# Issuing two of a rotation kernel's three stores from ACT instead of SyncE

## The chip, the cores and the metric

The kernel runs on one core of one Trainium2 chip. The metric is the device time of one execution in microseconds. The kernel before took 121.96 us in the median of three runs, from 121.85 to 122.02 us.

## The reference

A batch of 96 images (32 times 3 channels) of 256 x 256 float32 values is turned by 180 degrees: each image is reversed in both of its axes, which is the same as reversing its 65,536 values in order.

```python
batch, c, h, w = 32, 3, 256, 256
x = np.random.randn(batch, c, h, w).astype(np.float32)
return np.rot90(x, k=2, axes=(-2, -1)).astype(np.float32)
```

So 25.17 MB are read from DRAM, turned, and 25.17 MB written back. There is no arithmetic.

## The kernel before

The 96 images are taken as three groups of 32. In a group each image is cut into four parts of E = 16,384 values, so that a group is a tile of 128 partitions (image and part) by 16,384 values, 64 KB on each partition and 8.39 MB in all. Three such tiles, A, Bt and Ct, hold the three groups; each has a place of its own, so no tile is used twice. A fourth, T, of 2,048 values per partition, is scratch.

Turning an image is done in two steps. The order of the four parts is reversed by the access pattern of a DMA, and the values within a part are reversed by VectorE (DVE) in place:

- Group 0, tile A: loaded as it is, turned by DVE, stored with the parts reversed (`store`, L56 and L57). The load is in two pieces: the first 512 columns are issued by ACT, the other 15,872 by SyncE (both recorded on L54).
- Group 1, tile Bt: loaded with the parts reversed (L69), turned by DVE, stored as it is (L79).
- Group 2, tile Ct: loaded as it is (L54), turned by DVE, stored with the parts reversed (L57).

All loads are issued at the start, in the order A, Bt, Ct. `turn` walks from both ends of a tile to its middle and calls `swap` for each pair of pieces; `swap` makes three reversed or plain copies on DVE (recorded on L49): the right piece reversed into T, the left piece reversed into the right one's place, T into the left one's place. A and Ct are turned in 4 such steps of 2,048 columns, which makes 12 copies each; Bt in 6 steps of 1,366 columns (the last of 1,362), which makes 18. The copies stay in the order of the program.

The order of the stores is that of the program too: Bt's store first, then A's, then, after the turn of Ct, Ct's. Each engine's queue is in order: an instruction that issues a DMA waits on its engine for the semaphores of the copies and loads that it needs, and whatever stands behind it on that engine waits as well. Each engine that issues DMAs has a queue of its own on the 16 DMA engines: the profile's q1 has the bytes that SyncE issued, its q10 those that ACT issued. The scheduling framework (Tile) puts in the semaphores, and the waits at the program's end, recorded on L108.

Of the kernel before, what the change touches and what calls it, by code (L numbers as in the profile page):

```python
# [2 lines left out]

os.environ.setdefault("NEURON_RT_ULTRASERVER_MODE", "4")

# [4 lines left out]


@with_exitstack
def kernel(
    ctx: ExitStack,
    tc: tile.TileContext,
    x: bass.AP,
    out: bass.AP,
):
    nc = tc.nc  # L20
    P = 128

    B, C, H, W = x.shape
    L = H * W
    G = 32
    E = L // 4
    J = E // 8

    x4 = x.rearrange("b c h w -> (b c) (h w)").rearrange(
        "(g n) (s e) -> g (n s) e", n=G, s=4)  # L30
    o4 = out.rearrange("b c h w -> (b c) (h w)").rearrange(
        "(g n) (s e) -> g n s e", n=G, s=4)

    xr = x.rearrange("b c h w -> (b c) (h w)").rearrange(
        "(g n) (s e) -> g n s e", n=G, s=4)
    of = out.rearrange("b c h w -> (b c) (h w)").rearrange(
        "(g n) (s e) -> g (n s) e", n=G, s=4)

    pool = ctx.enter_context(tc.tile_pool(name="slots", bufs=1))
    A = pool.tile([P, E], x.dtype, tag="A")  # L40
    Bt = pool.tile([P, E], x.dtype, tag="B")
    Ct = pool.tile([P, E], x.dtype, tag="C")
    T = pool.tile([P, J], x.dtype, tag="T")

    def back(t, lo, hi):
        return t[:, hi - 1:(lo - 1 if lo else None):-1]

    def copy(dst, src):
        c = nc.vector.tensor_copy(out=dst, in_=src)  # L49
        tc.keep_in_program_order(c)  # L50
        return c

    def load(t, g, lo=0, hi=E, queue=nc.sync):
        return queue.dma_start(out=t[:, lo:hi], in_=x4[g][:, lo:hi])  # L54

    def store(t, g):  # L56
        return nc.sync.dma_start(out=o4[g][:, ::-1, :], in_=t[:, :])  # L57

    def swap(t, lo, w):
        hi = E - lo - w  # L60
        copy(T[:, 0:w], back(t, hi, hi + w))
        copy(t[:, hi:hi + w], back(t, lo, lo + w))
        copy(t[:, lo:lo + w], T[:, 0:w])

    half = E // 2

    load(A, 0, 512, E)
    load(A, 0, 0, 512, nc.scalar)
    nc.sync.dma_start(out=Bt[:, :], in_=xr[1][:, ::-1, :])  # L69
    load(Ct, 2)  # L70

    def turn(t, pieces):
        step = -(-half // pieces)
        for lo in range(0, half, step):
            swap(t, lo, min(step, half - lo))

    turn(A, 4)
    turn(Bt, 6)
    nc.sync.dma_start(out=of[1], in_=Bt[:, :])  # L79
    store(A, 0)  # L80
    turn(Ct, 4)
    store(Ct, 2)


# [1 line left out]
_INS = ['x']  # L86
_OUTS = [((32, 3, 256, 256), 'float32')]


# [23 lines left out]
```

## Time and profile before

| | us |
|---|---|
| median of three runs | 121.96 |
| the profiled execution's own time | 121.85 |
| its span, from first to last instruction | 120.1 |
| DVE busy, in 42 copies | 45.2 |
| idle time of DVE before its first copy of A, of Bt, of Ct | 22.6, 4.3, 3.1 |

The span holds 1,008 DMA packets and 50.33 MB, in the mean 419 GB/s. The profile's page lists the busy share of each engine, the span in 40 slices (each digit is the busy share of a slice in tenths), the DMA queues, and each DMA issue with the time from its issue to its landing. A row of the timeline gives start and duration, engine, line, operation, and in brackets the idle time before it with what ended that. "SPq" and "ACTq" are the instruction queues of SyncE and ACT, which issue DMAs. The trace also has a record of each single DMA packet, with its start, duration, size and queue.

### The profile page before, as it was taken

The page shows a single profiled execution, that of the slowest core. Times are in us where ns is not written, and L with a number is a line of the kernel's source. Part 1 is how long each engine was busy: PE and PEld are TensorE (multiplying, and loading weights), DVE is VectorE, ACT ScalarE, POOL GpSimd, SP SyncE. Part 2 cuts the span into 40 slices and gives each one's busy share as a digit, 9 for nine tenths or more (in the row PEclk, how much of TensorE's full clock was granted, in tenths as well). Part 3 has the DMA queues.
Part 4 walks back from the last instruction along what each step waited for, and adds up shares of the span by engine and source line. Part 5 has one row for each costly group of instructions (what it writes and reads, how often), then busy time and mean ns, then how long its engine had stood idle before and what let it go on. Part 6 is the DMA issues. An engine that isn't in the chain of part 4 may idle for free.

```text
span 120.1 us, 100 instructions
## 1 busy us (share of the span) xinstructions
DVE 45.2 (38%) x42; POOL 0.2 (0%) x4
## 2 busy tenths in 40 slices
DVE  0000000499995099999459999400000000000000
POOL 0000000000000000000000000000000000000000
DMA  9888988898889988998899889988998889888980
GB/s 338 349 349 351 697 349 349 360 677 371 349 349 633 415 349 349 590 459 349 349 524 524 349 349 480 568 349 349 415 633 349 349 371 677 349 349 371 655 371 0
DMA packets 1008, 50.33 MB, mean 419 GB/s; under 512 B 112, under 2 KB 112, under 8 KB 240
## 3 DMA queue, kind: packets, MB, share of 16 engines
q1 hardware_dynamic: 864, 50.07, 96.9%
q10 hardware_dynamic: 144, 0.26, 0.6%
HBM read 25.17 MB, written 25.17 MB: 419 GB/s over the span
## 4 chain that ended last, share of the span: by engine, by line
DMA 34%; DVE 26%; another core or an unknown queue 3%; issue 1%; SPq 0%; DVEq 0%
DMA Bt<-in_x_dram 34%; DVE Bt L49 9%; DVE T L49 9%; DVE Ct L49 8%; SPq L54 0%; DVEq L49 0%
## 5 line engine op out<-in xcount | busy, mean ns | idle before, releaser
L49 DVE COPY T<-A 128x2048 f32<-128x2048 f32 x4 | 4.9, 1226 | 22.7 <-DMA A<-in_x_dram 22.6
L49 DVE COPY T<-Bt 128x1366 f32<-128x1366 f32 (+1 forms) x6 | 5.2, 874 | 4.5 <-DMA Bt<-in_x_dram 4.3
L49 DVE COPY T<-Ct 128x2048 f32<-128x2048 f32 x4 | 4.9, 1227 | 3.2 <-DMA Ct<-in_x_dram 3.1
L49 DVE COPY Bt<-T 128x1366 f32<-128x1366 f32 (+1 forms) x6 | 5.2, 873 | 0.2
L49 DVE COPY Bt<-Bt 128x1366 f32<-128x1366 f32 (+1 forms) x6 | 5.2, 872 | 0.2
L49 DVE COPY Ct<-T 128x2048 f32<-128x2048 f32 x4 | 4.9, 1227 | 0.1
L49 DVE COPY A<-T 128x2048 f32<-128x2048 f32 x4 | 4.9, 1227 | 0.1
L49 DVE COPY A<-A 128x2048 f32<-128x2048 f32 x4 | 4.9, 1227 | 0.1
L49 DVE COPY Ct<-Ct 128x2048 f32<-128x2048 f32 x4 | 4.9, 1227 | 0.1
L97 POOL MEMSET const-bfloat16-1.0<- 128x1 bf16 x1 | 0.1, 101 | 0.0
L97 POOL MEMSET const-uint8-127<- 128x1 uint8 x1 | 0.1, 101 | 0.0
L97 POOL MEMSET const-float32-0.0<- 128x1 f32 x1 | 0.1, 98 | 0.2 <-issue 0.2
L97 POOL MEMSET const-float32-1.0<- 128x1 f32 x1 | 0.1, 98 | 0.0
## 6 DMA issues: line engine op xcount, KB each, us to landing
A<-in_x_dram SPq DMA_DIRECT2D x1, 7936.0 KB, 21.8
A<-in_x_dram ACTq DMA_DIRECT2D x1, 256.0 KB, 22.0
Bt<-in_x_dram SPq DMA_DIRECT2D x1, 40.8
Ct<-in_x_dram SPq DMA_DIRECT2D x1, 59.5
out_dram<-Bt SPq DMA_DIRECT2D x1, 22.3
out_dram<-A SPq DMA_DIRECT2D x1, 41.2
out_dram<-Ct SPq DMA_DIRECT2D x1, 42.7
```

Source lines behind the costliest of these rows:

```text
L49: c = nc.vector.tensor_copy(out=dst, in_=src)
L97: nc = _bacc.Bacc("TRN2", target_bir_lowering=False, num_devices=1)
```

## The change

`store` gets a parameter for the issuing engine, with SyncE as the default. The stores of Bt (group 1) and A (group 0) are issued by ACT (`nc.scalar`) in place of SyncE (`nc.sync`). Order, shapes and access patterns of the transfers stay as they are, and the loads and Ct's store stay on their engines.

```diff
-    def store(t, g):
-        return nc.sync.dma_start(out=o4[g][:, ::-1, :], in_=t[:, :])
+    def store(t, g, queue=nc.sync):
+        return queue.dma_start(out=o4[g][:, ::-1, :], in_=t[:, :])
...
     turn(A, 4)
     turn(Bt, 6)
-    nc.sync.dma_start(out=of[1], in_=Bt[:, :])
-    store(A, 0)
+    nc.scalar.dma_start(out=of[1], in_=Bt[:, :])
+    store(A, 0, nc.scalar)
     turn(Ct, 4)
     store(Ct, 2)
```

## The prediction

> **What bounds the kernel now.** I read the page first: its slices, its queues and its list of DMA issues.
>
> ```profile
> DVE  0000000499995099999459999400000000000000
> ...
> DMA  9888988898889988998899889988998889888980
> ...
> q1 hardware_dynamic: 864, 50.07, 96.9%
> q10 hardware_dynamic: 144, 0.26, 0.6%
> ```
>
> DVE is idle for 62% of the span; the 16 DMA engines are busy in all slices but the last, and their two queues (q1 is SyncE's, q10 ACT's, by their bytes) fill 97.5% of the span. I then read the single packet records in the trace, which the page only counts. A full packet is 65,536 B (one partition row) and takes 2.418 us; loads and stores take the same, but for some 15 ns more on a few loads. Each engine moves 8 rows in each of six transfers, so 48 x 2.418 = 116.1 us of the 120.1 us span. Followed on one engine, packets start 2.414 us apart from 4.7 us to 118.4 us without a gap. What lies outside is 1.7 us until the first packet, 0.7 us that the first packet takes longer, and some 1.6 us from the last packet to the end. So DMA work bounds the kernel from end to end, and a change moves the time only if it opens a gap in the packet stream, makes packets dearer, or alters the ends.
>
> ```profile
> A<-in_x_dram SPq DMA_DIRECT2D x1, 7936.0 KB, 21.8
> A<-in_x_dram ACTq DMA_DIRECT2D x1, 256.0 KB, 22.0
> Bt<-in_x_dram SPq DMA_DIRECT2D x1, 40.8
> Ct<-in_x_dram SPq DMA_DIRECT2D x1, 59.5
> out_dram<-Bt SPq DMA_DIRECT2D x1, 22.3
> out_dram<-A SPq DMA_DIRECT2D x1, 41.2
> out_dram<-Ct SPq DMA_DIRECT2D x1, 42.7
> ```
>
> The last column is from issue to landing. With the issue times of the timeline (0.72, 0.73, 1.16, 1.86, 58.33, 58.78, 76.53 us) the landings are at 22.57 and 22.74, then 41.9, 61.3, 80.65, 99.95 and 119.26 us: one transfer behind the other, 19.3 us each, and every store was issued well before its turn.
>
> Third, the timeline around the edit, and the waits of the SyncE queue.
>
> ```profile
> 57.43 0.87 DVE L49 COPY Bt<-T 128x1362 f32<-128x1362 f32 x1
> 58.33 0.35 SPq L79 DMA_DIRECT2D out_dram<-Bt  x1
> 58.78 0.61 SPq L57 DMA_DIRECT2D out_dram<-A  x1
> 61.40 1.23 DVE L49 COPY T<-Ct 128x2048 f32<-128x2048 f32 x1 [3.10 <-DMA Ct<-in_x_dram]
> ```
> ```profile
> SPq L79 <- DMA Bt<-in_x_dram: 39.4, 1, 39.4
> SPq L108 <- DMA out_dram<-Ct: 19.3, 1, 19.3
> SPq L108 <- DMA out_dram<-A: 19.3, 1, 19.3
> SPq L79 <- DVE Bt L49: 16.4, 1, 16.4
> SPq L57 <- DVE Ct L49: 15.2, 1, 15.2
> ```
>
> SyncE waits for tile Bt and its 18 copies, issues both stores back to back, and waits for Ct. Nothing that could run earlier stands behind these waits: the loads left by 2.5 us, and A, turned by 37.7 us, waits behind B in the same way after the change, in ACT's order.
>
> Fourth, what two queues do when both have packets. That happens once: in the load of A, whose first 512 columns go through ACT's queue.
>
> ```profile
> 4.60:7.00 2.40, 0.00 (x0) 0.00 (x0) 1.00 1.01 437
> ...
> 82.00:84.40 2.40, 0.00 (x0) 0.00 (x0) 1.00 1.01 437
> ```
>
> These are two stretches of one packet's length: in the first each engine starts one packet of each queue (63,488 B and 2,048 B), in the second one full packet of one queue. The rate, in the last column, is the same. By the records an engine alternates strictly, one packet from each queue: a pair takes 2.342 + 0.084 us less 8 ns of overlap, 2.418 us, against 2.414 us for one full packet.
>
> **The change, part by part.** *Issue.* Two DMA issues (0.35 and 0.61 us) and their waits move from SyncE to ACT. ACT has one issue of its own (0.39 us at 0.73 us, where SyncE's twin took 0.38) and is idle from then on, so the stores are issued at 58.33 and 58.78 us as before. Nobody is queued behind the new waits on ACT but these stores. SyncE is freed from 2.5 us on, but its only later issue is C's, which waits for DVE: gain nothing.
>
> *B's store overtakes the end of C's load.* From issue to first packet took 1.02 us at the start (0.72 to 1.74), so B's packets are ready at 59.35 us, while each engine is in its last packet of C's load (it ends at 60.33 to 60.95 us). C's completion packet (4 B) then finds another queue with work. Where this occurred in the load of A the engines alternated, so one B packet goes first: C lands 2.41 us later, at 63.7 instead of 61.3, DVE starts on Ct at 63.8 and C's store is issued at 78.94 instead of 76.53. Cost now: nothing, as B and A have packets queued until 99.1 us. C's store could come 19 us later before an engine ran dry. It is this cover that makes the delay free; without it 2.4 us would be paid.
>
> *C's store no longer queues behind A's.* C's first packets are ready at 78.94 + 1.02 = 79.96 us, and later by up to 0.3 us on the later engines. B's last packets end at 79.65 to 80.27 us in the same order of engines, so A goes first by some 0.3 us on each, and then A and C alternate: 16 packets per engine, as many as before, ending at the same 118.4 us. The price of alternating is taken from the load of A: nothing but the packets themselves, and there are no more of these.
>
> *The end.* Now two completion packets meet at the end of each engine: A's last data packet goes, then C's last, then A's completion, then C's. What that costs shows at 22 us, the only place where two completions meet: SyncE's 16 land 0.39 us (mean) after their 4 B packets start, ACT's, started 6 ns later, after 0.56 us, and the last of them 0.18 us after the last of SyncE's. The two landings of A, 22.57 and 22.74, are the two top rows of the issues. Completions of a single store took 0.39 to 0.45 us in the means. So the last landing is 0.18 us later. The sum: 0 + 0 + 0 + 0.18 us. For the ends of this term: 0 if the completions do not meet, and 0.27 if the lag grows with the store's completion (0.18 x 0.45/0.39 = 0.21) and SyncE's next wait, 0.06 us in the rows after its last one (119.28 to 119.35), follows it.
>
> The Trainium skill (DMA: Bandwidth & Descriptors, Queues, rings and completion order) says that a completion increment is a strongly ordered write that lands after every earlier write of its engine, across queues. That fits the second of two completions being late by 0.17 us here; it prices nothing by itself, and with it left out the term stays.
>
> The profiled execution took 121.85 us: its span of 120.1 and 1.8 outside. The median of the three runs is 121.96, 0.11 above. 121.85 + 0.18 = 122.03 for the former, and 122.14 us against the median: +0.15%. About 0.2% (0.24 us) is what a measurement of this kernel can tell from no change; the runs before spread over 0.17 us.
>
> **The rivals.** *1. The completions do not meet.* If an engine takes several packets from a queue before changing, C's completion follows its load directly, A's row of packets goes out whole, C's after it, and the end is as before: 121.96 us. The same comes out if C's packets enter ahead of A's and finish a packet early. Against it: the strict alternation in 16 packets on each engine in the load of A; for it: the 0.3 us margin above is small.
>
> The Trainium skill (same page and section) gives such a rule: an engine drains a whole packet of typically 9 to 17 descriptors from one queue before it changes. An engine's share of a transfer here is 8 rows and a completion, so by that rule A's share would go undivided. The records of the load of A, one row and then one row, speak against it.
>
> *2. Slower: alternating between two store queues costs something on each change.* No row shows two stores alternating, only two loads. From 80 us to 118 us there are 15 changes on each engine, all on the path. The nearest row sets the low end: no cost, at 5 to 22 us. The far end is an engine that starts cold: the first packet took 3.06 us in the median where the next ones of its size took 2.342, so 0.72 us x 15 = 10.8 us, 133 us. It decides from 0.24 / 15 = 16 ns per change. I take the near row for the forecast, since a load also reads one memory and writes another; for the range 35 ns, 0.53 us on top of the forecast, 122.7 us. The more likely part of this rival is that low part: single packets of stores are as steady as loads.
>
> *3. Faster: two queues hide what a packet costs beyond its bytes.* 2,048 B took 84 ns, where the step from 63,488 to 65,536 B took 76: 8 ns fixed, of which 4 are already overlapped. Hiding all of it in the 16 packets of the stage gives 0.13 us at most, 121.83, which would count as the same. A gain over 0.24 us needs something that no row shows.
>
> **How the numbers follow.** Forecast 0.58 (of it 0.16 above 0.2%, since its upper end is 0.27 us and the next measurement scatters); rival 1 0.16 (0.14 within, 0.01 on each side); rival 2 0.20, all slower; rival 3 and what I have not seen 0.06, faster. Together faster 0.07, same 0.56, slower 0.37. The range goes from 121.8, below rival 1 and the lowest of the runs, to 122.7, which leaves out the dear part of rival 2 (about 0.1) and the gain (0.05). The likeliest case's own range is 121.95 to 122.3.
>
> **What would show it.** Right: q10 with about 17.0 MB; B's store from ACT at 58.3, landing at 80.6; DVE's wait for Ct 5.5 instead of 3.1 us; C's store issued near 78.9; A and C landing within 0.3 us of each other near 119.3 and 119.45, so A at 60.5 us from its issue instead of 41.2 and C at 40.5; packets of 2.42 us throughout. Rival 1: A lands near 100. Rival 2: packets from 80 us on longer than 2.43 us, or gaps between them. A gap anywhere between 5 and 118 us would make the forecast wrong.

## The result: 132.49 us, slower by 8.7%

The changed kernel took 132.49 us in the median of four runs (132.35 to 132.99), the kernel before 121.92 us beside it. The ratio is 1.087, with a 95% interval from 1.084 to 1.090. The forecast was 122.14 us, in a range of 121.8 to 122.7: wrong by far.

The page of the changed kernel, with its slices and queues:

```profile
DVE  0000000999950999980000000000999950000000
...
DMA  8799799799799779998999998989989969898870
...
q1 hardware_dynamic: 576, 33.29, 63.0%
q10 hardware_dynamic: 432, 17.04, 31.2%
```

The bytes moved to ACT's queue as foreseen (17.04 MB on q10). But there is a hole of ten slices in DVE's row, some 33 us, where before Ct's turn followed Bt's at once. The list of the DMA issues, with the time from issue to landing in the last column, names the transfer:

```profile
A<-in_x_dram SPq DMA_DIRECT2D x1, 7936.0 KB, 22.0
A<-in_x_dram ACTq DMA_DIRECT2D x1, 256.0 KB, 22.2
Bt<-in_x_dram SPq DMA_DIRECT2D x1, 40.9
Ct<-in_x_dram SPq DMA_DIRECT2D x1, 89.5
out_dram<-A ACTq DMA_DIRECT2D x1, 53.6
out_dram<-Bt ACTq DMA_DIRECT2D x1, 52.1
out_dram<-Ct SPq DMA_DIRECT2D x1, 23.4
```

Ct's load needs 89.5 us where it needed 59.5, and A's store is now listed ahead of Bt's. The timeline says when they were issued:

```profile
37.91 0.62 ACTq L57 DMA_DIRECT2D out_dram<-A  x1
...
58.53 0.37 ACTq L79 DMA_DIRECT2D out_dram<-Bt  x1
...
91.41 1.23 DVE L49 COPY T<-Ct 128x2048 f32<-128x2048 f32 x1 [32.92 <-DMA Ct<-in_x_dram]
...
106.54 0.61 SPq L57 DMA_DIRECT2D out_dram<-Ct  x1
```

A's store leaves at 37.91 us, the moment A is turned, and not behind Bt's at 58.5. The scheduling framework orders each engine's instructions itself, and the code pins only the copies to the order of the program. On ACT it put the store first that is ready first; why it had kept the order of the program on SyncE, where A was ready just as early, is not shown. From 41 us on each engine therefore alternates between Ct's load (q1) and A's store (q10), and Ct lands at 91.3 instead of 61.3 us. DVE needs 15.1 us for it, and the store of Ct is issued at 106.54 us instead of 76.53.

By the packet records the eight loads and eight stores on each engine ought to end at 79.6 to 80.3 us, if each took 2.418 us. They end at 84.9 to 89.3 us on 15 engines and at 91.0 us on the last. Packets of Ct's load took 3.02 us in the mean, those of A's store 2.59, single ones up to 4.1. The slowest engine was never idle afterwards: Bt's eight packets until 110.3 us, Ct's until 129.6. So its loss of 11 us in the alternating stretch is the loss of the kernel. The faster engines end Bt's store from 104.2 us on and wait until 107.8 us for Ct's.

The stretch by windows (length, DVE, POOL, clock, DMA share, and GB/s by the packets started), in the changed kernel and then in the kernel before:

```profile
46.00:80.00 34.00, 12.05 (x14) 0.00 (x0) 1.00 0.99 372
```
```profile
46.00:80.00 34.00, 26.58 (x26) 0.00 (x0) 1.00 1.02 443
```

The share says busy in both, 0.99 and 1.02, while the rate is 372 against 443 GB/s. (Packets that start inside a window count whole; 16 engines with a packet of 65,536 B each 2.414 us make 434.) The busy share of DMA alone hides such a loss.

### The profile page after: what moved, and what is told of

The parts are those of the page before. It is cut to its first block, busy times and chain, and to the rows that moved or that the text cites. A ratio compares the mean times of both kernels' runs of the same rounds, so it can differ in the third digit from the quotient of the medians.

```text
span 130.7 us, 100 instructions
## 1 busy us (share of the span) xinstructions
DVE 45.2 (35%) x42; POOL 0.2 (0%) x4
## 3 DMA queue, kind: packets, MB, share of 16 engines
q10 hardware_dynamic: 432, 17.04, 31.2%
## 4 chain that ended last, share of the span: by engine, by line
DMA 31%; another core or an unknown queue 25%; DVE 24%; issue 1%; SPq 0%; DVEq 0%
DMA Bt<-in_x_dram 31%; DVE Bt L49 8%; DVE T L49 8%; DVE Ct L49 8%; SPq L54 0%; DVEq L49 0%
## 6 DMA issues: line engine op xcount, KB each, us to landing
Ct<-in_x_dram SPq DMA_DIRECT2D x1, 89.5
```

## The experiments

Theory 1, the order theory, was formed on the traces: the order did it; A's store went out early, beside Ct's load. Its rival: alternation between two queues is dear whatever they carry (the queue theory), as the prediction's second rival had it. Ratios are against the kernel before, run beside each.

### Bt's store first on ACT

```diff
     nc.scalar.dma_start(out=of[1], in_=Bt[:, :])
-    store(A, 0, nc.scalar)
+    tc.keep_in_program_order(store(A, 0, nc.scalar))
```

> Both stores on ACT, but with A's pinned behind Bt's, which is the order that the prediction took for granted. Order theory (the loss comes from A's store going out at 38 us, when Bt is still being turned, so that it shares the DMA engines with Ct's load): Ct lands at about 63.7 us, C's store is issued near 79 us, and the time is the forecast, 122.1 us (121.9 to 122.3). Queue theory (two queues that alternate are dear whatever they carry): A's and C's stores alternate from 80 to 118 us with packets of 2.8 to 3.1 us instead of 2.42, and the time is 127 to 133 us.

Measured: 122.85 us, ratio 1.0064 (1.0050 to 1.0077). Its DMA issues:

```profile
Ct<-in_x_dram SPq DMA_DIRECT2D x1, 59.7
out_dram<-Bt ACTq DMA_DIRECT2D x1, 25.5
out_dram<-A ACTq DMA_DIRECT2D x1, 61.2
out_dram<-Ct SPq DMA_DIRECT2D x1, 43.3
```

and their issue times:

```profile
58.63 0.35 ACTq L79 DMA_DIRECT2D out_dram<-Bt  x1
59.08 3.02 ACTq L57 DMA_DIRECT2D out_dram<-A  x1
...
76.78 0.61 SPq L57 DMA_DIRECT2D out_dram<-Ct  x1
```

With the order that the prediction took for granted, 9.7 of the 10.6 us are gone. A's and Ct's stores alternate here from 82 us on, and by the windows and records that is free: every packet from 84 to 116 us took 2.418 us.

```profile
84.00:116.00 32.00, 0.00 (x0) 0.00 (x0) 1.00 0.98 426
```

The queue theory falls for two stores. 0.88 us remain. The first packet of Bt's store, the first on q10 since 22 us, took 3.22 us in the mean over the engines instead of 2.42, which is 0.80 of it. The other 0.08 us is less than the runs scatter (122.75 to 122.92).

The long wait of the queue is not enough to make a first packet long: Ct's first store packets, the first on q1 since 61 us, took 2.418 us here, behind store packets, where Bt's first ones came behind load packets. In the changed kernel, though, four of Ct's first store packets, right behind the last of Bt's, took 2.63 to 3.27 us, so the cause of the 0.80 us stays open.

The two completions at the end added nothing. The last landings of the two stores are 0.19 us apart, but it is Ct's that came first (76.78 us and 43.3 make 120.1) and A's that came last (59.08 and 61.2 make 120.3). Ct landed at 61.56 us, in a run where Bt's load already landed 0.3 us later than before: no packet of Bt's store overtook its completion.

### One of the two stores at a time

Only A's store on ACT:

```diff
-    nc.scalar.dma_start(out=of[1], in_=Bt[:, :])
+    nc.sync.dma_start(out=of[1], in_=Bt[:, :])
     store(A, 0, nc.scalar)
```

> Only A's store moved to ACT; Bt's stays with SyncE. Order theory: A's store still goes out at 38 us and alternates with Ct's load from 41 us, Ct lands near 91 us and the time is 130 to 134 us. Bt's store then stands behind Ct's load in SyncE's queue, and starts when an engine has finished that load. If it is the number of stores on ACT that costs: about half of the 10.6 us, 127 us.

Measured: 132.20 us, ratio 1.0845 (1.0817 to 1.0872). A's store was issued at 37.68 us; from 41 to 84 us load packets took 3.02 and store packets 2.63 us in the mean. Moving A's store alone brings the loss.

Only Bt's store on ACT:

```diff
     nc.scalar.dma_start(out=of[1], in_=Bt[:, :])
-    store(A, 0, nc.scalar)
+    store(A, 0)
```

> Only Bt's store moved to ACT; A's stays with SyncE, where it is issued early but stands behind Ct's load in the same queue. Order theory: Ct lands by 64 us and the time is 121.9 to 122.3 us, though from 61 us on Bt's and A's stores alternate from two queues. Queue theory: 127 to 133 us, by the alternation of two stores for some 38 us.

Measured: 122.88 us, ratio 1.0068 (1.0055 to 1.0080). Bt's and A's stores alternated in packets of 2.418 us. But there was a miss: 0.9 us over the kernel before, and more than the order theory's 122.3. Here A's store waits in SyncE's queue from 38 us, and the last packet of Ct's load took 3.39 us in the mean.

### Two loads from two queues

```diff
-    load(Ct, 2)
+    load(Ct, 2, queue=nc.scalar)
```

This is an edit to the kernel before; all stores stay with SyncE.

> No store is moved; Ct's load is issued by ACT, so that two whole loads (Bt's and Ct's) alternate from 22 to 61 us in packets of 65,536 B. If any alternation of two queues is dear: packets of 2.8 to 3.1 us, and Bt lands at 66 us or later. If it is dear only when one queue loads while the other stores: packets of 2.42 us, and both land at 61 us.

Measured: 122.97 us in one run. Two loads alternate at full rate, 2.422 us a packet in the mean from 25 to 57 us:

```profile
26.00:57.00 31.00, 11.52 (x10) 0.00 (x0) 1.00 1.02 440
```

So what the load of A showed holds for large packets of one direction, and what it could not show is a load beside a store. Here too the last packets of Ct's load (on ACT's queue), with a store waiting on SyncE's, were long: 3.67 us in the mean. And SyncE now issued A's store ahead of Bt's, since nothing pins their order:

```profile
37.85 0.60 SPq L57 DMA_DIRECT2D out_dram<-A  x1
...
78.81 0.36 SPq L79 DMA_DIRECT2D out_dram<-Bt  x1
```

### A's store first, all on SyncE

```diff
     turn(A, 4)
+    tc.keep_in_program_order(store(A, 0))
     turn(Bt, 6)
-    nc.sync.dma_start(out=of[1], in_=Bt[:, :])
-    store(A, 0)
+    tc.keep_in_program_order(nc.sync.dma_start(out=of[1], in_=Bt[:, :]))
```

> The kernel before, with all stores on SyncE, but A's issued ahead of Bt's, at 38 us. If the early issue alone did the harm, Ct would land late and the time be 130 us or more. If the harm needs the second queue: A's packets stand behind Ct's load in the one queue, Ct lands at 61.3 us, and the time is 121.9 to 122.1 us.

Measured: 122.92 us, ratio 1.0077 (1.0062 to 1.0092). The early issue without the second queue does not delay Ct by A's bytes, which stand behind it (Ct landed at 62.5). But 1.0 us was lost where nothing was expected. The last packet of Ct's load took 3.57 us in the mean, on all 16 engines, in a single queue; in the kernel before 2.44.

### The same order, with the store issued late

```diff
-    turn(A, 4)
-    turn(Bt, 6)
-    nc.sync.dma_start(out=of[1], in_=Bt[:, :])
-    store(A, 0)
+    turn(A, 6, 0, 5)
+    turn(Bt, 6, 0, 5)
+    turn(A, 6, 5, 6)
+    tc.keep_in_program_order(store(A, 0))
+    turn(Bt, 6, 5, 6)
+    tc.keep_in_program_order(nc.sync.dma_start(out=of[1], in_=Bt[:, :]))
```

Here `turn(t, pieces, first, last)` does the steps from first up to last alone; A is turned in six steps here instead of four.

> All stores on SyncE and A's first, as in the kernel that lost 1.0 us by it, but A's last step of copies is put behind the fifth of Bt's six, so that A's store is issued at 58.3 us, where Bt's was before, when each engine is already in its last packet of Ct's load. If the 1.0 us is the price of a store that already waits in the queue when the last load packet starts: it is gone, load and store packets around 60 us take 2.42 us, and the time is 121.9 to 122.1 us. If it is the price of A's store as the first one, or of the order: 122.9 us and a last load packet of 3.6 us.

Measured: 121.88 us, ratio 0.9994 (0.9985 to 1.0003). A's store, issued at 58.32 us, behind the same load in the same queue, costs nothing: the last load packets took 2.42 us. So the 1.0 us is paid by a load packet that starts while a store already waits behind it. A store that arrives in the load's own queue during the last load packet is free; from the other queue, in the run with Bt's store first on ACT, its own first packet was long instead. The kernel before had the free case, by the time at which Bt's turn ends.

### Smaller packets in the changed kernel

Here the order theory is tested from the other side, on the changed kernel: A's store stays early and beside Ct's load, and only the sizes change. Both in quarters (the halves are made in the same way, with 2 and 8192):

```diff
-    load(Ct, 2)
+    for q in range(4):
+        load(Ct, 2, 4096 * q, 4096 * q + 4096)
...
-    store(A, 0, nc.scalar)
+    for q in range(4):
+        nc.scalar.dma_start(out=o4[0][:, ::-1, 4096 * q:4096 * q + 4096],
+                            in_=A[:, 4096 * q:4096 * q + 4096])
```

> The changed kernel, with Ct's load and A's store cut into quarters of the columns, so that the two queues alternate in packets of 16 KB: 32 loads and 32 stores per engine, 64 handovers instead of 16, for the same bytes. If the loss is a price per handover (0.33 us on the fastest engine to 0.7 us on the slowest, from 5.2 and 11.3 us over 16): 21 to 45 us are lost, Ct lands at 101 to 125 us, and the time is 142 us or more. If loads and stores in flight together only move their bytes more slowly, by a share that does not depend on the packets: Ct lands near 91 us and the time stays at 130 to 134 us.

Measured: 131.14 us in one run, and the total fits the second theory by accident. The packets fit neither: from 44 to 79 us all loads and stores took 0.611 us, their full rate, with 64 handovers. The time went elsewhere. Once A's store was through, Bt's packets of 64 KB took turns with Ct's last quarter in packets of 16 KB, so Ct landed at 91.7 us all the same (near the second theory's 91, for another reason), and the engines stood idle from 101 us (Bt's store done) to 108 us.

In halves:

> The changed kernel, with Ct's load and A's store cut into halves of the columns, packets of 32 KB, between the 64 KB that lost 5 to 11 us in alternation and the 16 KB that lost nothing. If the loss has a threshold in the packet's size: either packets of 1.21 us throughout, or packets lengthened on many engines as with 64 KB. Bt's store then competes in packets of 64 KB in either case, so that the total says little; the packets from 45 to 60 us say it.

Measured: 123.26 us in one run, and all packets of 32 KB took 1.213 us from 44 to 80 us. The windows show the stretch that stood at 372 GB/s in the changed kernel:

```profile
46.00:80.00 34.00, 14.20 (x17) 0.00 (x0) 1.00 1.01 435
```

All of it in quarters, Bt's store too:

```diff
-    nc.scalar.dma_start(out=of[1], in_=Bt[:, :])
+    for q in range(4):
+        nc.scalar.dma_start(out=of[1][:, 4096 * q:4096 * q + 4096],
+                            in_=Bt[:, 4096 * q:4096 * q + 4096])
```

> The changed kernel with its order kept (A's store ahead on ACT, at 38 us), but Ct's load and both stores on ACT in quarters of the columns, packets of 16 KB. If the loss comes from alternating loads and stores in packets of 64 KB: packets of 0.61 us without gaps, Ct lands near 84 us, C's store is ready near 100 us, about when Bt's store ends (99.5 us), and the time is 122.5 to 124.5 us: most of the 10.6 us is gone, though A's store is as early as before. If delaying Ct's load by A's bytes is the loss by itself, whatever the packets: 130 us or more.

Measured: 123.80 us, ratio 1.0152 (1.0135 to 1.0169), with packets of 0.611 us and Ct landed at 84.3 us. So order theory as first put is not enough: A's store 20 us early, and Ct late by 23 us, cost less than 2 us as long as the packets are short. The early store opens the stretch; the loss of 10.6 us comes with packets of 64 KB. Of the 1.35 us that the run with halves still lost, 1.07 are the first change from load to store: the last packet of Bt's load took 3.48 us in the mean.

### Which packet has to be long

Only Ct's load in halves, A's store in 64 KB:

```diff
-    load(Ct, 2)
+    for q in range(2):
+        load(Ct, 2, 8192 * q, 8192 * q + 8192)
```

> The changed kernel with only Ct's load in halves (packets of 32 KB), A's store in packets of 64 KB. If the long load packet is what loses: load packets of 1.21 us and store packets of 2.42 us from 45 us on. If the long store packet is: store or load packets lengthened by 0.3 to 1 us there. In either case Bt's long packets then share with the rest of Ct's load, so Ct lands near 99 us and the total, near 137 us, tells nothing.

Measured: 151.57 us in one run. Store packets took 2.85 us in the mean from 45 to 105 us, and loads 1.35 instead of 1.21:

```profile
46.00:96.00 50.00, 12.05 (x14) 0.00 (x0) 1.00 1.00 374
```

Ct landed at 112.6 us, past the 99 us expected, since its 16 packets now stood beside 16 long ones.

Only A's store in halves, Ct's load in 64 KB:

```diff
-    store(A, 0, nc.scalar)
+    for q in range(2):
+        nc.scalar.dma_start(out=o4[0][:, ::-1, 8192 * q:8192 * q + 8192],
+                            in_=A[:, 8192 * q:8192 * q + 8192])
```

> The changed kernel with only A's store in halves (packets of 32 KB), Ct's load in packets of 64 KB. If the long load packet is what loses: load packets of 2.7 to 4 us from 45 us on and Ct lands past 75 us. If the long store packet is: load packets of 2.42 us and store packets of 1.21 us, Ct lands near 71 us, and the time is 122 to 124 us.

Measured: 123.30 us in one run, loads of 2.418 and stores of 1.217 us:

```profile
46.00:70.00 24.00, 14.44 (x17) 0.00 (x0) 1.00 0.99 429
```

This one cut, with the stores on ACT and in the changed order, takes away more than nine of the 10.6 us. The long packet that hurts is the store's. Each of these two kernels ran once; the gap between 151.57 and 123.30 us is far beyond the scatter of the others. Cutting a store by columns also makes two DMAs of it and changes the order in which it writes DRAM, and no run tells these from the length of the packet.

### Changes of direction on one queue

A's store and Ct's load in 8 column pieces each on SyncE's queue, in turn (`cols(k)` is the k-th eighth of the columns; A is loaded by SyncE alone, with its parts reversed, and stored as it is):

```diff
+    for k in range(8):
+        tc.keep_in_program_order(nc.sync.dma_start(out=of[0][:, cols(k)], in_=A[:, cols(k)]))
+        tc.keep_in_program_order(nc.sync.dma_start(out=Ct[:, cols(k)], in_=x4[2][:, cols(k)]))
```

> Everything on SyncE's one queue, but A's store and Ct's load are cut into 8 column pieces each and issued in turn (store, load, store, load), so that an engine changes between storing and loading every 64 KB, as in the changed kernel, without a second queue. A's parts are reversed in its load instead of its store. Two-queue theory (a change of direction costs only when it goes to the other queue, for then the next packet isn't started under the one before): the stretch from 41 us takes 38.7 us, packets of 8 KB at 0.30 us, Ct lands near 80 us, C's store is issued near 96 us while Bt's is still running, and the time is 122 to 123 us. Direction theory (loads and stores in turn on an engine are dear in any queue): the stretch takes 44 to 50 us, Ct lands at 85 to 91 us, and the time is 127 to 133 us.

> The control of the alternating kernel: the same 16 pieces on one queue, all loads of Ct first and then all stores of A. Both theories: no change of direction but one, Ct lands near 61 us, and the time is 122 to 123 us. What it has above 122.0 is the price of the pieces.

Measured: 125.36 us, ratio 1.0283 (1.0260 to 1.0306), and 123.59 us, ratio 1.0134 (1.0118 to 1.0149), for the control. Neither theory's range has the 125.36. The stretch of 16 pieces took 39.9 us in the mean over the engines with 15 changes of direction inside it, and 39.8 us with the control's one. So changes between packets of 8 KB cost next to nothing. The first change, from Bt's load, cost more: the last packet of that load took 3.46 us in the mean, 2.42 in the control. The control's only change, from 8 KB loads to 8 KB stores, cost 0.4 to 0.5 us. Since packets of 16 KB turned out to lose nothing on two queues either, this pair doesn't decide on the queue.

The same alternation in rows, 16 rows of 64 KB in one DMA (`t[k::8]`), with Bt's store cut likewise:

> One queue only: A's store and Ct's load are cut by partitions into 8 DMAs of 16 rows each, one packet of 65,536 B per engine, issued in turn, so that engines change between store and load at every 64 KB packet without a second queue. Bt's store is cut in the same way and shows what such DMAs cost in one direction. If alternating 64 KB packets of loads and stores is dear in any queue: packets of 2.5 to 4 us from 41 to 85 us, above those of Bt's store. If it needs two queues: the same packet times in both stretches.

Measured: 158.85 us in one run, inconclusive. Bt's store, one direction and nothing beside it, took up to 5.4 us a packet when cut in this way, so these row DMAs are slow by themselves.

Three changes of direction on one queue, with whole transfers:

```diff
-    load(Ct, 2)
...
     turn(A, 4)
+    tc.keep_in_program_order(store(A, 0))
+    tc.keep_in_program_order(load(Ct, 2))
     turn(Bt, 6)
     nc.sync.dma_start(out=of[1], in_=Bt[:, :])
-    store(A, 0)
```

> All on SyncE's one queue, in the order load A, load Bt, store A, load Ct, store Bt, store Ct: three changes between loading and storing in 64 KB packets, each with the next transfer already waiting in the queue, and no second queue. If each such change costs about 1.0 us, as the one in the kernel with A's store early on SyncE did: 124 to 125 us, and the packets at each change (near 41, 61 and 80 us) are 0.7 to 1.3 us longer. If only a change from load to store costs: 124 us, with the change near 61 us (store to load) free. If one queue pays only once: 123 us.

Measured: 123.02 us, ratio 1.0080 (1.0063 to 1.0097). The change near 41 us, from load to store, lengthened the load packet ahead of it to 3.12 us in the mean. The one near 61 us, from store to load, was free but on one engine (2.75 us). The one near 80 us, to Bt's store, cost between nothing and 0.7 us, unevenly over the engines, 0.18 in the mean. So a single queue pays too, once for a change from load to store, and not each time the same. What it would pay if it changed at every packet of 64 KB is not shown.

## Why the prediction was wrong, step by step

- **What bounds the kernel** held: DMA from end to end, and only a gap, dearer packets or the ends can move the time. Packets did become dearer, and the page's busy share did not show it.
- **The issue step failed first.** "A, turned by 37.7 us, waits behind B in the same way after the change, in ACT's order" took the order of the code for the order of the queue. The measured issue is at 37.91 us, not at 58.78. SyncE's order before was the program's, but nothing pins it, for only the copies are kept in order; in the run with two loads SyncE too issued A's store ahead of Bt's (37.85 and 78.81 us). With the order pinned the time is 122.85 us.
- **The price of alternating failed with it.** "The price of alternating is taken from the load of A: nothing but the packets themselves". For two loads and for two stores that is right (2.42 us each). For a load beside a store in 64 KB packets it is 0.60 us per load packet and 0.17 us per store packet in the mean, 11 us over 16 packets on the slowest engine. This term decides: with the true order and the free price, by an estimate from the packets of 2.418 us, A's store and Ct's load would have ended near 80 us, Ct's store would have been ready near 97 us, while Bt's ran until 99, and nothing would have been lost. The runs with short store packets come close to that, at 123.3 us, of which about 1.0 is the last packet of Bt's load (3.36 and 3.48 us in the mean).
- **The second rival** had the far end of a price, 10.8 us, and so a total of 133 us that is near the measured one. That is chance: it placed the cost between two stores at the end, which is free.
- **B's store overtaking C's completion** did not occur where the order was as assumed: Ct landed within 0.3 us of before.
- **The end** came out by number alone, in the run with Bt's store first on ACT: 0.19 us between the last landings, for 0.18 forecast, but in the other order. Where the two completions met, on 13 engines, the second did land late, as forecast: Ct's came 0.55 us after their packets in the mean of all 16, A's 0.40. But on the three engines that ended last Ct's packets had gone ahead of A's, which is what rival 1 allowed for, and A's completion there ended the kernel with nothing added.
- **A term was missing even in the assumed order:** the first packet of Bt's store, on a queue that had been idle and after a load packet of the other queue, 0.80 us. With it, and without the 0.18 us of the end, 121.97 us becomes 122.77, for 122.85 measured. The nearest row, the first packet of the program with 3.06 us for 2.34, was in the prediction, but as the far end of a rival about two stores.
- **One reading was too smooth:** "loads and stores take the same, but for some 15 ns more on a few loads". Two of the last packets of Ct's load took 2.49 and 2.59 us, the one place where a store came behind a load in the kernel before.

The Trainium skill (DMA: Bandwidth & Descriptors, Issuing engines are not separate DMA queues) says that DMAs from several engines share the same 16 DMA engines and interleave, and that issuing from more than one saves issue time alone. The records agree with the first part, and show a price that goes beyond it: 372 GB/s in the interleaved stretch.

## What to carry to other kernels

Moving a DMA to another engine's queue removes the order that the old queue gave for nothing: read the new queue's order in the timeline, or pin it, before pricing anything. When a store can overtake into a stretch of loads, price the stretch by rate and not by the busy share, and try the store's rows cut to 32 KB, not the load's alone (123.30 against 151.57 us). Where DMA is the bound, a store that is issued just in time behind the last load, in the same queue, can beat one that waits there early.

## What was not expected of the hardware

- Two queues that alternate load and store packets of 65,536 B run at 372 GB/s instead of 434; with store packets of 32,768 B or less they lose nothing after the first change from load to store. Why the length of the store's packet decides is open.
- A store that already waits when the last load packet starts lengthens that packet by 0.7 to 1.2 us in the means of the runs, in one queue as in two (by 0.18 us only at the second such change of the run with three); one that arrives during it, in the same queue, doesn't (121.88 against 122.92 us). The mechanism is open too.
- Turns go by packet, not by bytes: 16 KB packets of Ct's load beside 64 KB packets of Bt's store left the load a fifth of the time.
- In the run with Bt's store first on ACT, A's issue behind it held ACT for 3.02 us (0.62 in the changed kernel). Nothing waited for it.
